# Moving activations and normed activations to other start addresses modulo 512 bytes

## The chip, the cores and the metric

The kernel runs on one core of a Trainium2 chip. The metric is the time of the kernel on the device, in microseconds (us). Before the change three runs took 1006.5, 1007.32 and 1007.83 us; the median is 1007.32.

SBUF, the on-chip memory, has 128 partitions. A tile of 128 x 512 numbers of 4 bytes takes 2048 bytes in each partition, and its address is the place of its first byte in the partition, the same in all 128. The change is about these addresses.

## The reference

A decoder trunk of two layers on 512 positions and 1024 channels, all in float32:

```
x = x + multiscale_pool(rmsnorm(x))           # layer 0
x = x + conv_ffn(rmsnorm(x))
k, v = split(rmsnorm(x, kv_norm) @ w_kv)      # layer 1
x = x + diff_attention(rmsnorm(x), k, v)
x = x + conv_ffn(rmsnorm(x))
return rmsnorm(x, final_norm)

def conv_ffn(h):                              # 1024 -> 2 x 2816 -> 1024
    u = causal_dwconv(h @ w_up)               # width 3
    a, g = split(u)
    return (silu(g) * a) @ w_down
```

The two feed-forward parts hold most of the arithmetic: each multiplies 512 x 1024 by 1024 x 5632 and 512 x 2816 by 2816 x 1024.

## The kernel before

A float32 product is made of three products of halves: every operand is split into a high part that TensorE's one-pass format (fp32r) holds exactly and a low part with the rest, and `mm3` (L159 to L163) adds high x high (L161), high x low (L162) and low x high (L163) into one PSUM bank. In `nc.tensor.matmul(ps, l, r)` the operand `l` is stationary: its 128 columns are loaded into the array by a weight load (PEld in the profile). `r` is moving: its columns stream through. In the profile's names, `pu<-n1h,hi_u`, the moving operand stands first and the stationary one second.

The stages, in order, with the tiles of their matmuls:

- Pooling of layer 0 (`dps`, `pp`): 128 and 256 columns.
- Up projections (`pu`, in `product`): for each of 44 blocks of 128 channels, 8 x 3 matmuls; the weights `hi_u`, `lo_u` are stationary, the normed, transposed activations `n1h`, `n1l` (layer 1: `n3h`, `n3l`) move, 512 columns each. The first four blocks are computed in two halves of 256 columns.
- Down projections (`pd`, in `ffn`): the activations `ah`, `al` are stationary, the weights `hi_d`, `lo_d` move, 512 columns each.
- Attention: values `pv` (weights move, normed activations `n2h`, `n2l` are stationary), queries and keys `pj_q`, `pj_k` (weights stationary, normed activations move), scores `sc`, transposes `pa`, weighted values `po`, output projection `pw` (weights move, activations `oh`, `ol` stationary).

Weights come in chunks of 512 KB: a DMA on SP's queue into `raw` (three buffers), ScalarE's copy into `hi`, VectorE's subtraction into `lo` (five buffers each). The order of the instructions of each engine is the order in which the code issues them; the early part follows a written list of steps (`ORDER`).

Tiles come from pools, which take space in SBUF in the order in which they are opened. With the sizes of their tiles this gives the addresses, in bytes in the partition:

| pool | what is in it | starts at | its tiles modulo 512 |
|---|---|---|---|
| start | `ones`, 896 bytes | 1152 | 128 |
| tp | 44 tiles of 2048 bytes: activations `ah`, `al`, `oh`, `ol`, `qs`, `kh`, `kl`, `v`, pooling operands | 2048 | 0 |
| hp | 2 tiles of 16384 bytes: normed activations | 92160 | 0 |
| wp | 13 tiles of 4096 bytes: weights `raw`, `hi`, `lo` | 124928 | 0 |
| const | x, identity, gains | 178176 | x and identity 0 |
| work | scratch | 196928 | 2048-byte tiles 0, 4096-byte tiles 320 |

Every matmul operand in tp, hp and wp is a slice that begins a multiple of 512 bytes into its tile (128 columns of 4 bytes, or more). So it has its tile's residue modulo 512: before the change 0 for both operands of every product that `mm3` makes.

Of the kernel before, what the change touches and what calls it, by code (L numbers as in the profile page):

```python
# [8 lines left out]
F32 = mybir.dt.float32  # L9
# [5 lines left out]
P = 128  # L15
# [48 lines left out]
def trunk(ctx, tc, x, norm_g, pool_w, pool_scale, kv_norm, w_kv, wq, lam, subln_g, wo,  # L64
          w_up, conv_w, conv_b, w_down, final_norm, consts, out):
    nc = tc.nc

    start = ctx.enter_context(tc.tile_pool(name="start", bufs=1))
    tp = ctx.enter_context(tc.tile_pool(name="tp", bufs=1))
    hp = ctx.enter_context(tc.tile_pool(name="hp", bufs=1))  # L70
    wp = ctx.enter_context(tc.tile_pool(name="wp", bufs=1))
    const = ctx.enter_context(tc.tile_pool(name="const", bufs=1))
    work = ctx.enter_context(tc.tile_pool(name="work", bufs=1))
    ones = start.tile([P, 224], F32, name="ones")
    psum = ctx.enter_context(tc.tile_pool(name="psum", bufs=8, space=bass.MemoryType.PSUM))
    ctx.enter_context(tc.manual_schedule(engines={mybir.EngineType.PE}))

# [59 lines left out]
    for i in (1, 2):  # L137
        n = S if i == 1 else 64
# [623 lines left out]
```

## Time and profile before

| | |
|---|---|
| median of three runs | 1007.32 us |
| profiled execution | 1007.95 us |
| its span | 1006.2 us |
| granted TensorE clock, mean | 0.999 |
| PE busy | 991.4 us, 99% |
| weight loads (PEld) busy | 838.3 us, 83% |
| VectorE, ScalarE, GpSimd busy | 569.7, 426.9, 85.7 us |
| DMA, mean | 95 GB/s |

The page of the profile gives shares over the whole span. A busy PE says little, since matmuls overlap: a row's duration runs from the start to a modelled end, and the next one has started long before. What a matmul costs in a row of matmuls is the distance from its start to the next start. The timeline has the starts, and the table by stretches the counts.

### The profile page before, as it was taken

The numbers are of one execution on the slowest core, as the hardware profiler recorded it, in microseconds if no ns is written. First come the engines' busy times: TensorE is split into PE (matmuls) and PEld (weight loads), VectorE is DVE, ScalarE is ACT, GpSimd is POOL, SyncE is SP. The second block draws the span as 40 slices with busy tenths as digits, with TensorE's granted clock in tenths as the row PEclk, the third lists the DMA queues.
The fourth block names the chain that finished last, engine by engine and source line by source line (L and its number), as shares of the span: only waits on it lengthen the run. The fifth ranks groups of instructions, "written<-read, shape, count | busy, mean of one in ns | idle before, by whom it ended". The sixth has DMA issues, their size and how long they took to land.

```text
span 1006.2 us, 12339 instructions
## 1 busy us (share of the span) xinstructions
PE 991.4 (99%) x4870; PEld 838.3 (83%) x4870; DVE 569.7 (57%) x872; ACT 426.9 (42%) x671; POOL 85.7 (9%) x113
## 2 busy tenths in 40 slices
PE   8999999999999999999999999999999999999997
PEld 8998888888888888778888887988888888888885
DVE  5766656656632323557766797576566566532213
ACT  5554443444432213446756662464444434422211
POOL 4500000000000001261220101000000000000001
PEclk9999999999999999999999999999999999999999
DMA  7333233233232321243213111243332332332312
GB/s 259 109 105 105 85 104 101 88 105 94 94 110 85 114 98 49 71 139 105 64 42 105 64 43 42 84 126 95 94 105 88 101 104 85 105 94 95 105 42 83
DMA packets 128707, 95.33 MB, mean 95 GB/s; under 512 B 3329, under 2 KB 111498, under 8 KB 128650
## 3 DMA queue, kind: packets, MB, share of 16 engines
q1 hardware_dynamic: 128650, 94.55, 30.4%
q8 instruction: 38, 0.62, 0.2%
q14 instruction: 19, 0.16, 0.0%
HBM read 92.44 MB, written 2.10 MB: 94 GB/s over the span
## 4 chain that ended last, share of the span: by engine, by line
PE 96%; DVE 1%; DMA 1%; ACT 0%; issue 0%; SPq 0%; POOL 0%; DVEq 0%; POOLq 0%; ACTq 0%
PE pu L161 16%; PE pu L162 16%; PE pu L163 16%; PE pd L163 8%; PE pd L161 8%; PE pd L162 8%; PE sc L531 2%; PE po L560 2%; PE pw L163 1%; PE pj_k L161 1%; PE pj_k L162 1%; PE pw L162 1%; PE pw L161 1%; PE pj_k L163 1%; PE pj_q L162 1%; PE pj_q L161 1%
## 5 line engine op out<-in xcount | busy, mean ns | idle before, releaser
L144 DVE TENSOR_TENSOR lo_u<-raw_u,hi_u 128x1024 fp32r<-128x1024 f32 x84 | 103.3, 1232 | 126.9 <-ACT hi_u L143 126.7
L161 PE MATMUL pu<-n3h,hi_u 128*128 128x512 f32 (+1 forms) x384 | 142.9, 372 | 0.0
L161 PE MATMUL pu<-n1h,hi_u 128*128 128x512 f32 (+1 forms) x384 | 142.8, 372 | 0.0
L162 PE MATMUL pu<-n3l,hi_u 128*128 128x512 f32 (+1 forms) x384 | 142.6, 371 | 0.0
L162 PE MATMUL pu<-n1l,hi_u 128*128 128x512 f32 (+1 forms) x384 | 142.6, 371 | 0.0
L163 PE MATMUL pu<-n1h,lo_u 128*128 128x512 f32 (+1 forms) x384 | 142.6, 371 | 0.0
L163 PE MATMUL pu<-n3h,lo_u 128*128 128x512 f32 (+1 forms) x384 | 142.6, 371 | 0.0
L144 DVE TENSOR_TENSOR lo_d<-raw_d,hi_d 128x1024 fp32r<-128x1024 f32 x44 | 53.9, 1226 | 147.1 <-ACT hi_d L143 147.1
L161 PE MATMUL pd<-hi_d,ah 128*128 128x512 f32 x352 | 137.0, 389 | 0.0
L163 PE MATMUL pd<-hi_d,al 128*128 128x512 f32 x352 | 136.9, 389 | 0.0
L162 PE MATMUL pd<-lo_d,ah 128*128 128x512 f32 x352 | 136.9, 389 | 0.0
L143 ACT CAST hi_u<-raw_u 128x1024 fp32r<-128x1024 f32 x84 | 88.1, 1051 | 64.2 <-PE pu L162 59.4
L143 ACT CAST hi_d<-raw_d 128x1024 fp32r<-128x1024 f32 x44 | 46.2, 1050 | 142.0 <-PE pd L163 131.3
L161 PEld LDWEIGHTS pu<-n1h,hi_u 128*128 128x128 f32 x384 | 72.3, 188 | 12.6
L163 PEld LDWEIGHTS pu<-n3h,lo_u 128*128 128x128 f32 x384 | 72.3, 188 | 12.6
L163 PEld LDWEIGHTS pu<-n1h,lo_u 128*128 128x128 f32 x384 | 72.3, 188 | 12.5
L162 PEld LDWEIGHTS pu<-n3l,hi_u 128*128 128x128 f32 x384 | 72.4, 188 | 12.5
L161 PEld LDWEIGHTS pu<-n3h,hi_u 128*128 128x128 f32 x384 | 72.3, 188 | 12.4
L162 PEld LDWEIGHTS pu<-n1l,hi_u 128*128 128x128 f32 x384 | 72.4, 188 | 12.3
L162 PEld LDWEIGHTS pd<-lo_d,ah 128*128 128x128 f32 x352 | 66.1, 188 | 13.7
L163 PEld LDWEIGHTS pd<-hi_d,al 128*128 128x128 f32 x352 | 66.1, 188 | 13.7
L161 PEld LDWEIGHTS pd<-hi_d,ah 128*128 128x128 f32 x352 | 66.1, 188 | 13.6
(146 smaller groups left out, 1553.2 us busy)
## 6 DMA issues: line engine op xcount, KB each, us to landing
raw_u<-in_w_up_dram SPq DMA_DIRECT2D x88, 512.0 KB, 3.7
raw_d<-in_w_down_dram SPq DMA_DIRECT2D x44, 512.0 KB, 3.3
raw_v<-in_w_kv_dram SPq DMA_DIRECT2D x8, 512.0 KB, 3.6
raw_q<-in_wq_dram SPq DMA_DIRECT2D x8, 512.0 KB, 4.0
raw_k<-in_w_kv_dram SPq DMA_DIRECT2D x8, 512.0 KB
raw_o<-in_wo_dram SPq DMA_DIRECT2D x8, 512.0 KB, 4.9
x<-in_x_dram SPq DMA_DIRECT2D x4, 512.0 KB
out_dram<-y SPq DMA_DIRECT2D x8, 256.0 KB, 2.1
```

Of the source, the lines that this page charges most:

```text
L143: nc.scalar.copy(hi, src)
L144: nc.vector.tensor_tensor(lo, src, hi, ALU.subtract)
L161: nc.tensor.matmul(ps, lh, rh, start=first, stop=False)
L162: nc.tensor.matmul(ps, lh, rl, start=False, stop=False)
L163: nc.tensor.matmul(ps, ll, rh, start=False, stop=last)
L531: nc.tensor.matmul(ps[:, :m], qs[h, c][:, q], k[:, :m], start=not last, stop=bool(last))
L560: nc.tensor.matmul(po[h][:, qi * P:(qi + 1) * P], aT[:, kt * P:(kt + 1) * P], vt[kt][h // 4][:, (h % 4) * VD:(h % 4 + 1) * VD], start=kt = ...
```

## The change

The pools are opened in another order, and two pools of one tile each stand between them: 256 bytes (64 numbers) and 288 bytes (72 numbers). The two tiles are filled with zeros on GpSimd, and nothing reads them.

```diff
     start = ctx.enter_context(tc.tile_pool(name="start", bufs=1))
+    wp = ctx.enter_context(tc.tile_pool(name="wp", bufs=1))
+    gap1 = ctx.enter_context(tc.tile_pool(name="gap1", bufs=1))
     tp = ctx.enter_context(tc.tile_pool(name="tp", bufs=1))
+    gap2 = ctx.enter_context(tc.tile_pool(name="gap2", bufs=1))
     hp = ctx.enter_context(tc.tile_pool(name="hp", bufs=1))
-    wp = ctx.enter_context(tc.tile_pool(name="wp", bufs=1))
     const = ctx.enter_context(tc.tile_pool(name="const", bufs=1))
     work = ctx.enter_context(tc.tile_pool(name="work", bufs=1))
     ones = start.tile([P, 224], F32, name="ones")
+    for pool, n in ((gap1, 64), (gap2, 72)):
+        nc.gpsimd.memset(pool.tile([P, n], F32, name="gap"), 0.0)
```

The addresses after it: wp at 2048 (0 modulo 512), tp at 55552 (256), hp at 145952 (32), const at 178720 (x and identity 32), work at 197472 (its 2048-byte tiles 32, its 4096-byte tiles 352). For the products this means:

| product | moving, from | stationary, from | before, moving / stationary | after |
|---|---|---|---|---|
| pu, pj_q, pj_k | hp | wp | 0 / 0 | 32 / 0 |
| pv | wp | hp | 0 / 0 | 0 / 32 |
| pd, pw | wp | tp | 0 / 0 | 0 / 256 |
| pp, sc | tp | tp | 0 / 0 | 256 / 256 |
| po | tp | work | 0 / 0 | 256 / 32 |

The instructions of PE, VectorE, ScalarE and SP are the same in the same order, with the same waits. Only GpSimd's row of instructions changes, at its beginning. Before:

```order
L757 UNCONDITIONAL_BRANCH
L109 MEMSET halfneg 128x8
L181 ISA
L181 TENSOR_SCALAR r_n_150<-ssq_n_148 128x1
L184 TENSOR_TENSOR r_n_150<-r_n_150,halfneg 128x1
```

And after it (`gap` are the new tiles, `halfneg` a constant for the power -0.5, `r_n` the factor of the first normalization; the lines are 5 further down):

```order
L762 UNCONDITIONAL_BRANCH
L79 MEMSET gap 128x64
L79 MEMSET gap 128x72
L114 MEMSET halfneg 128x8
L186 ISA
L186 TENSOR_SCALAR r_n_160<-ssq_n_158 128x1
```

The two fills stand ahead of the fill of `halfneg`; the rest follows as before.

## The prediction

> **What bounds the kernel now.** I read the page first: the share of each engine and the chain that ended last.
>
> ```profile
> span 1006.2 us, 12339 instructions
> PE 991.4 (99%) x4870; PEld 838.3 (83%) x4870; DVE 569.7 (57%) x872; ACT 426.9 (42%) x671; POOL 85.7 (9%) x113
> ...
> PE 96%; DVE 1%; DMA 1%; ACT 0%; issue 0%; SPq 0%; POOL 0%; DVEq 0%; POOLq 0%; ACTq 0%
> ```
>
> TensorE sets the end: 96% of the chain is matmuls following each other on PE. So the time is the number of matmuls times the distance from one start to the next, plus little else. Next the table by stretches, for two long stretches: first the up projections of layer 0, then its down projections (columns: stretch, PE busy and count, weight loads, DVE, ACT, POOL, granted clock, DMA share, GB/s).
>
> ```profile
> 70.00:290.00 220.00, 220.00 (x973) 182.21 (x972) 134.47 (x167) 94.81 (x121) 0.00 (x0) 1.00 0.32 97
> 290.00:385.00 95.00, 95.00 (x421) 78.69 (x420) 24.49 (x24) 19.48 (x20) 0.00 (x0) 1.00 0.31 103
> ```
>
> PE is never idle, the granted clock is full (1.00), DVE is busy 61% of the first stretch (134.47 of 220) and 26% of the second, ACT 43% and 21%, DMA a third. Nothing else is near a limit. The count gives the distance of starts: 220/973 = 226 ns and 95/421 = 226 ns (a matmul that straddles an edge is counted too). The timeline gives it exactly. The first and last rows stand here of 19 matmuls of 512 columns, and then 22 of 256 columns:
>
> ```profile
> 199.78 0.39 PE L162 MATMUL pu<-n1l,hi_u 128*128 128x512 f32 x1
> ...
> 203.86 0.39 PE L162 MATMUL pu<-n1l,hi_u 128*128 128x512 f32 x1
> ```
> ```profile
> 59.05 0.28 PE L162 MATMUL pu<-n1l,hi_u 128*128 128x256 f32 x1
> ...
> 61.57 0.28 PE L162 MATMUL pu<-n1l,hi_u 128*128 128x256 f32 x1
> ```
>
> 18 steps in 4.08 us are 226.7 ns each; 21 steps in 2.52 us are 120.0 ns each. (The 389 ns in the groups is one matmul's length from start to modelled end; neighbours overlap, so it is not what one costs.) The two sizes separate a part per column from a part per matmul: (226.7 - 120.0)/256 = 0.417 ns a column, and 226.7 - 512 x 0.417 = **13.3 ns per matmul that does not depend on its columns**. All the change can win lies in these 13.3 ns.
>
> What are they? One thing happens once per matmul whatever its width: the next stationary block, 128 columns of 4 bytes, is read from SBUF while the moving operand is read. The timeline shows both starting together:
>
> ```profile
> 200.24 0.39 PE L161 MATMUL pu<-n1h,hi_u 128*128 128x512 f32 x1
> 200.24 0.19 PEld L162 LDWEIGHTS pu<-n1l,hi_u 128*128 128x128 f32 x1
> ```
>
> So two streams leave SBUF at the same moment, and before the change both begin at 0 modulo 512. Whether they get into each other's way is the open question; no matmul of 256 columns or more in this trace has its two operands at different residues, so the trace can't answer it directly. One thing speaks for it. The distance isn't a constant of the array: after each pause of a stream it is longer for a while, with the same tiles. Eight starts just after a group of score matmuls:
>
> ```profile
> 520.50 0.39 PE L162 MATMUL pv<-lo_v,n2h 128*128 128x512 f32 x1
> 520.73 0.40 PE L163 MATMUL pv<-hi_v,n2l 128*128 128x512 f32 x1
> 520.97 0.39 PE L161 MATMUL pv<-hi_v,n2h 128*128 128x512 f32 x1
> 521.20 0.40 PE L162 MATMUL pv<-lo_v,n2h 128*128 128x512 f32 x1
> 521.43 0.39 PE L163 MATMUL pv<-hi_v,n2l 128*128 128x512 f32 x1
> 521.66 0.39 PE L161 MATMUL pv<-hi_v,n2h 128*128 128x512 f32 x1
> 521.89 0.39 PE L162 MATMUL pv<-lo_v,n2h 128*128 128x512 f32 x1
> 522.12 0.39 PE L163 MATMUL pv<-hi_v,n2l 128*128 128x512 f32 x1
> ```
>
> Seven steps in 1.62 us are 231.4 ns, 4.7 over the settled 226.7. An overhead that depends on how two streams stand to each other in time is what a clash at the memory looks like, and a shift of addresses acts on the same thing. A fixed cost of changing the weights would not do this.
>
> **The change part by part.** It adds two fills on GpSimd, moves addresses, and leaves the instructions of all other engines as they are, in the same order with the same waits.
>
> (a) The two fills stand ahead of the fill of halfneg on POOL:
>
> ```profile
> 0.72 0.10 POOL L109 MEMSET halfneg<- 128x8 f32 x1 [0.29 <-POOLq L745]
> 5.45 0.22 POOL L181 TENSOR_SCALAR r_n<-ssq_n 128x1 f32<-128x1 f32 x1 [4.63 <-ACT sq_n L191]
> ```
>
> POOL then idles 4.63 us for the first row of x, so two fills of 64 and 72 columns, at the 0.10 us of an 8-column one or even at several times that, are hidden by that wait. Without it they would cost some 0.2 us. I take 0.
>
> (b) The tensors other than TensorE's operands (x, the gains, scratch) begin 32 bytes later. VectorE and ScalarE keep their work; if they became a few per cent slower, the 39% and 57% that they have free in the up stretch would hold it. I take 0.
>
> (c) The matmuls whose two operands now differ modulo 512. Their counts, from the groups by line with shapes kept apart:
>
> ```profile
> L161 PE MATMUL pd<-hi_d,ah 128*128 128x512 f32 x352 | 137.0, 389 | 0.0
> L161 PE MATMUL pu<-n1h,hi_u 128*128 128x512 f32 x320 | 124.5, 389 | 0.0
> L161 PE MATMUL pw<-hi_o,oh 128*128 128x512 f32 x64 | 25.6, 400 | 0.8 <-ACT oh L148 0.8
> L161 PE MATMUL pv<-hi_v,n2h 128*128 128x512 f32 x64 | 25.2, 394 | 0.0
> L161 PE MATMUL pj_k<-n2h,hi_k 128*128 128x512 f32 x64 | 25.0, 391 | 0.0
> L161 PE MATMUL pj_q<-n2h,hi_q 128*128 128x512 f32 x64 | 25.0, 390 | 0.0
> L161 PE MATMUL pu<-n1h,hi_u 128*128 128x256 f32 x64 | 18.3, 286 | 0.0
> ```
>
> Each row stands three times (the three products of the hi and lo halves), and pu in both layers. That makes pu 2 x 3 x 320 = 1920 of 512 columns and 2 x 3 x 64 = 384 of 256, with the moving operand 32 bytes off; pj_k and pj_q 384, likewise 32; pv 192, where the stationary one is 32 off; pd 3 x 352 = 1056 and pw 192, where the stationary one is 256 off. Together 4128. The pooling products and the scores have both operands in the activations' pool: their relation stays 0, and I take 0 for them. The small attention products and transposes are paced by their weight loads (below), and I take 0.
>
> What does one of the 4128 gain? The lower end of the gain is nothing, or less (a rival below). The upper end comes from the transposes, 128 columns each:
>
> ```profile
> 32.22 1.75 PE pt_n L226 x16
> ```
>
> 1.75/16 = 109.4 ns each, where 128 columns at 0.417 would need 53: here the weight load sets the pace, so one load takes at most 109.4 ns. A matmul of 256 columns can't follow faster than its weight load and so gains at most 120.0 - 109.4 = 10.6 ns, and I take this end for 512 columns too, since the overhead was the same. Between 0 and 10.6 no row decides; I take half of the 13.3, 6.7 ns, as if the two streams met half as often. The settled distance would be 220.0 ns.
>
> As to the skill: in "TensorE: Matmul & The Clock Gate", section "Back-to-back issue gap", the Trainium skill gives N/2.4 + 2.5 ns for one matmul after another. By that figure an estimate of the distance is 215.8 ns at 512 columns and 109.2 at 256, the gain 10.9 x 3744 + 10.8 x 384 = 45 us and the time 962 us. The trace agrees with its part per column (0.417), not with its constant (13.3 against 2.5).
>
> The sum: pu 1920 x 6.7 ns = 12.9 us; pd 1056 x 6.7 = 7.1; pj, pv and pw 768 x 6.7 = 5.1; pu with 256 columns 384 x 6.7 = 2.6. Together 27.7 us. The profiled execution took 1007.95 us (its span 1006.2 and 1.75 around it), which is 0.6 over the median of 1007.32. 1007.95 - 27.7 = 980.2; against the median **979.6 us**. With the upper end it is 4128 x 10.6 = 43.8 us, or 963.5.
>
> Would something else become the bound at 220 ns? Everything that runs beside a matmul stays the same in total: DVE's 134.47 us would stand in a stretch of 213.5 instead of 220, 63%. No.
>
> **The rivals.**
>
> 1. *Addresses don't matter; the 13.3 ns is the price of swapping weights.* For it: in the settled rhythm 226.7 is the same in the up and the down stretch, though moving and stationary tiles change places there. Against it: the 231.4. The time is 1007.3. The Trainium skill speaks for this rival: "TensorE: Matmul & The Clock Gate", section "Step-by-step: what each phase is for", says that TensorE reads the moving operand and the weights through two separate SBUF ports, and that loading the next weights takes nothing from the running matmul. By that rule the change does nothing. No row here contradicts it outright; the shifting distance makes me doubt it.
>
> 2. *Only one shift helps.* The normed activations move by 32 bytes, the others by 256, so the two groups can differ. If only the 256 helps (pd and pw, 1248): 1248 x 6.7 = 8.4 us, 998.9. If only the 32 helps (pu, pj and pv, 2880): 19.3 us, 988.0. For it: a shift of 32 bytes is a small part of the 512 bytes that a weight load reads. Against it: no row tells the two apart.
>
> 3. *Slower: the streams no longer settle.* That the distance falls back to 226.7 after a pause may need equal residues. If the streams with shifted operands stay in the state that they have after a pause, each of the 4128 takes 4.7 ns more: 19.4 us, 1026.7. If only pd and pw do (1248): 5.9 us, 1013.2. It decides once the mean distance is over 227.2 ns (2 us over 4128 matmuls). For it: 231.4 occurs, over and over. Against it: it is always a passing state.
>
> **How the numbers follow.** Within 0.2% (2 us) a change of this kernel can't be told from none. I give the forecast, both shifts help by something up to 10.6 ns, 0.38; rival 2, 0.20; rival 1, 0.25; rival 3, 0.17. Faster is 0.38 + 0.20 = 0.58, same 0.25, slower 0.17. The forecast's own range is 962 to 993 (a gain of 3.5 to 11 ns each). To hold 8 in 10 the range takes in rivals 2 and 1 and the smaller form of rival 3: 962 to 1013; left out are the larger form of rival 3 (about 0.11) and a gain beyond the upper end (0.04). The likeliest case gives 979.6, rounded 980.
>
> **What would show it.** In the profile after, starts of pu with 512 columns 220.0 ns apart (18 steps in 3.96 us), those of 256 columns 113.3, and pd the same 220.0; the up stretch then holds about 3% more matmuls in the same time. Scores and pooling products keep their distance. Rival 1 would show 226.7 everywhere; rival 2 one of pu and pd at 226.7 and the other below it; rival 3 one of them over 227.2 for a whole stage. The sum would be wrong if PE showed new idle time ahead of the matmuls, or if the time moved while the distances did not.

## The result: slower, and only where the shift is 32 bytes

The changed kernel takes 1020.5 us (median of four runs), the kernel before beside it 1006.91: a ratio of 1.013, with an interval of 1.0115 to 1.0144. That is 13.6 us more. The forecast was 27.7 us less.

The profile after, first the page:

```profile
span 1018.2 us, 12341 instructions
...
PE 1006.1 (99%) x4870; PEld 836.3 (82%) x4870; DVE 568.2 (56%) x872; ACT 427.4 (42%) x671; POOL 86.2 (8%) x115
...
PE 97%; DVE 1%; DMA 1%; SPq 0%; issue 0%; ACT 0%; DVEq 0%; POOLq 0%; POOL 0%; ACTq 0%
```

The kernel is bound as before; no new wait has come up. The table by stretches, for the same two stretches:

```profile
70.00:290.00 220.00, 220.00 (x945) 176.84 (x944) 131.25 (x161) 92.01 (x118) 0.00 (x0) 1.00 0.32 96
290.00:385.00 95.00, 95.00 (x421) 78.67 (x420) 25.45 (x28) 21.10 (x22) 0.00 (x0) 1.00 0.30 99
```

The columns are those of the prediction's table. In 220 us the up projections now get through 945 matmuls; it was 973. The down projections get through 421, as before. PE is full in both and the granted clock is 1.00, so the matmuls of `pu` themselves stand further apart. The timeline has the distance: first and last of 19 `pu` matmuls of 512 columns, of 19 `pd` matmuls, and of 20 `pu` matmuls of 256 columns.

```profile
199.70 0.39 PE L168 MATMUL pu<-n1h,lo_u 128*128 128x512 f32 x1
...
203.90 0.39 PE L168 MATMUL pu<-n1h,lo_u 128*128 128x512 f32 x1
...
329.79 0.39 PE L167 MATMUL pd<-lo_d,ah 128*128 128x512 f32 x1
...
333.87 0.39 PE L167 MATMUL pd<-lo_d,ah 128*128 128x512 f32 x1
```
```profile
58.66 0.28 PE L167 MATMUL pu<-n1l,hi_u 128*128 128x256 f32 x1
...
60.87 0.28 PE L168 MATMUL pu<-n1h,lo_u 128*128 128x256 f32 x1
```

18 steps of `pu` in 4.20 us are 233.3 ns (before 226.7). 18 steps of `pd` in 4.08 us are 226.7, unchanged. 19 steps of 256 columns in 2.21 us are 116.3 (116.6 by the starts in ns; before 120.0). So where the 32 bytes were put, the matmuls of 512 columns became slower and those of 256 faster, and where the 256 bytes were put, nothing changed. That the shift is the cause is what the experiments below test.

The loss adds up. From all starts in the two traces (distances with a wait or pause in them left out), 1920 `pu` matmuls of 512 columns take 6.6 ns more each, 12.7 us; 576 of `pj_q`, `pj_k` and `pv` go from 228.0 to 233.1 on average, 2.9 us; 384 `pu` matmuls of 256 columns go from 119.9 to 117.0, 1.1 us less. Together 14.5 us, against 13.6 measured (11.6 to 14.5 by the interval). The spans of the two traces differ by less, 12.0 us, because waits of PE differ too: before, PE is idle for 1.9 us ahead of `pv<-hi_v,n2l`, and in the trace after for none. Of the kernels below that keep the time of before, two have this wait (1.6 and 1.9 us) and one has 0.1, so it is not the change's.

### The profile page after: what moved, and what is told of

Same layout as the page of the kernel before. It is cut to its first block, busy times and chain, and to the rows that moved or that the text cites. A ratio compares the mean times of both kernels' runs of the same rounds, so it can differ in the third digit from the quotient of the medians.

```text
span 1018.2 us, 12341 instructions
## 1 busy us (share of the span) xinstructions
PE 1006.1 (99%) x4870; PEld 836.3 (82%) x4870; DVE 568.2 (56%) x872; ACT 427.4 (42%) x671; POOL 86.2 (8%) x115
## 4 chain that ended last, share of the span: by engine, by line
PE 97%; DVE 1%; DMA 1%; SPq 0%; issue 0%; ACT 0%; DVEq 0%; POOLq 0%; POOL 0%; ACTq 0%
PE pu L166 16%; PE pu L167 16%; PE pu L168 16%; PE pd L168 8%; PE pd L167 8%; PE pd L166 8%; PE sc L536 2%; PE po L565 2%; PE pv L168 1%; PE pw L168 1%; PE pv L167 1%; PE pj_k L167 1%; PE pj_k L166 1%; PE pv L166 1%; PE pj_k L168 1%; PE pw L166 1%
```

## The experiments

Theory A: what counts is how the moving and the stationary operand stand to each other modulo some power of two; 32 bytes is a bad relation, 256 is as good as 0. The rivals: the loss comes from the activations at 256 or from the scratch that moved along (B); an operand that begins at 32 is read more slowly by itself (C); traffic of the other engines makes the difference (D). The first six kernels are edits of the kernel before, all with the same means: the order of the pools, gaps between them and the size of the first tile. The code shown leaves out the lines that fill the gaps; its comments are added.

### The normed activations alone at 32

```diff
     start = ctx.enter_context(tc.tile_pool(name="start", bufs=1))
+    wp = ctx.enter_context(tc.tile_pool(name="wp", bufs=1))
     tp = ctx.enter_context(tc.tile_pool(name="tp", bufs=1))
+    gap1 = ctx.enter_context(tc.tile_pool(name="gap1", bufs=1))     # 8 numbers, 32 bytes
     hp = ctx.enter_context(tc.tile_pool(name="hp", bufs=1))
-    wp = ctx.enter_context(tc.tile_pool(name="wp", bufs=1))
```

> Weights and activations at 0 modulo 512, normed activations alone at 32. Theory A (what counts is how the moving operand stands to the stationary one that is loaded meanwhile; only the 32 hurts): pu, pj and pv of 512 columns at 233 ns as after the change, pd and pw at 226.7, pu of 256 columns at 117; about 1020 us, the whole loss. Theory B (the loss comes from the activations at 256, or from scratch and constants that moved with them): under 1010 us. Both have scratch and constants 32 bytes off here as after the change, so a loss here with nothing else doesn't yet separate A from a shift of scratch; the next kernel does.

1021.63 us, ratio 1.0142 (1.0125 to 1.0159). The timeline of this kernel, first and last of 19 matmuls each:

```profile
199.69 0.39 PE L166 MATMUL pu<-n1h,lo_u 128*128 128x512 f32 x1
...
203.89 0.39 PE L166 MATMUL pu<-n1h,lo_u 128*128 128x512 f32 x1
...
329.77 0.39 PE L165 MATMUL pd<-lo_d,ah 128*128 128x512 f32 x1
...
333.85 0.39 PE L165 MATMUL pd<-lo_d,ah 128*128 128x512 f32 x1
```

`pu` at 4.20/18 = 233.3 ns, `pd` at 226.7: the whole loss is here. Scratch and constants stand 32 bytes further on here too, as after the change; the third kernel takes up that rival.

### The activations alone at 256

```diff
+    wp = ctx.enter_context(tc.tile_pool(name="wp", bufs=1))
+    gap1 = ctx.enter_context(tc.tile_pool(name="gap1", bufs=1))     # 256 bytes
     tp = ctx.enter_context(tc.tile_pool(name="tp", bufs=1))
+    gap2 = ctx.enter_context(tc.tile_pool(name="gap2", bufs=1))     # 256 bytes
     hp = ctx.enter_context(tc.tile_pool(name="hp", bufs=1))
-    wp = ctx.enter_context(tc.tile_pool(name="wp", bufs=1))
```

> Activations at 256, normed activations and weights at 0, scratch and constants at the residues they had before the change. Theory A: nothing slower, pd at 226.7 ns, pu at 226.7, 1007 us within 2. Theory B (the 256 costs): 1013 us or more, although pd already kept 226.7 in the changed kernel.

1007.01 us, ratio 0.9996 (0.9982 to 1.0009). Its stretches hold the counts of the kernel before:

```profile
70.00:290.00 220.00, 220.00 (x973) 182.15 (x972) 135.76 (x168) 96.25 (x123) 0.00 (x0) 1.00 0.33 97
290.00:385.00 95.00, 95.00 (x421) 78.67 (x420) 23.60 (x22) 18.53 (x19) 0.00 (x0) 1.00 0.32 103
```

Theory B falls as far as the 256 bytes go.

### Everything 32 bytes later

```diff
-    ones = start.tile([P, 224], F32, name="ones")
+    ones = start.tile([P, 232], F32, name="ones")
```

(with the pools in the order start, wp, tp, hp)

> Everything 32 bytes later: weights, activations and normed activations all at 32 modulo 512, so the relation of every pair of operands is 0 as before the change. Theory A (relation of the two): pu and pd at 226.7 ns, 1007 us within 2. Theory C (an operand that begins off a boundary of 64 or more bytes is read more slowly by itself): pu at 233 and pd above 226.7 too, about 1027 us.

1006.08 us, ratio 0.9989 (0.9977 to 1.0).

```profile
70.00:290.00 220.00, 220.00 (x973) 182.15 (x972) 134.44 (x167) 95.05 (x121) 0.00 (x0) 1.00 0.33 97
```

973 again. An operand at 32 is not slow by itself, and scratch and constants, which moved by 32 here too, cost nothing: theory C falls, and the rest of B. What counts is how the two operands stand to each other, their relation.

### Three other places

The gap ahead of `hp` of the first experiment, with 16 numbers (64 bytes) in place of 8:

> The normed activations at 64 modulo 512, weights and activations at 0. If the streams alone (relation 64: 229.05 ns at 512 columns, 117.75 at 256; relation 192, which pv has: 233.35) give the kernel's time: pu 1920 x 2.4 ns = 4.5 us, pj 384 x 1.5 = 0.6, pv 192 x 5 = 1.0, the 256-column products 384 x -2.2 = -0.9; together +5.2, 1012 us. If any shift off 0 costs the same as 32: 1021.

1013.07 us, ratio 1.005 (1.0031 to 1.0068): +5.0 us, where the streams alone (below) had said +5.2.

```profile
70.00:290.00 220.00, 220.00 (x963) 180.53 (x962) 134.08 (x167) 95.37 (x123) 0.00 (x0) 1.00 0.32 97
```

The same gap with 64 numbers (256 bytes):

> The normed activations at 256, weights and activations at 0. From the streams alone (relation 256: 226.6 ns at 512 columns, 120 at 256): pu at 226.7, 1007 us within 2. If normed activations off 0 are slow whatever the shift: 1020.

1007.96 us, ratio 1.0008 (0.9996 to 1.0021).

```profile
70.00:290.00 220.00, 220.00 (x973) 182.23 (x972) 134.90 (x168) 95.16 (x122) 0.00 (x0) 1.00 0.32 97
```

The normed activations can be moved by 256 bytes without loss; it is the 32, and less the 64, that hurts.

And the pools in the order start, wp, hp, a gap of 8 numbers, tp, so that the 32 bytes stand between the operands of `pd` and `pw`:

> The activations at 32, weights and normed activations at 0: the 32 bytes now sit between the operands of pd and pw. From the streams alone (stationary 32 off: 233.3 ns): pd 1056 x 6.6 ns = 7.0 us, pw 192 x 5 = 1.0; 1015 us, pu at 226.7. If the loss belongs to the normed activations and not to the 32 bytes: 1007.

1013.95 us, ratio 1.0078 (1.0056 to 1.0101): +7.9 by the ratio, 7.2 by the medians (8.0 expected). The stretches show that the loss has moved to the down projections:

```profile
70.00:290.00 220.00, 220.00 (x971) 182.08 (x970) 135.42 (x168) 95.66 (x123) 0.00 (x0) 1.00 0.32 97
290.00:385.00 95.00, 95.00 (x408) 76.59 (x408) 23.61 (x22) 18.18 (x18) 0.00 (x0) 1.00 0.29 97
```

408 matmuls of `pd` in place of 421: 95/408 = 233 ns.

### The streams by themselves

A kernel that leaves the trunk out: it loads x, makes one large moving and one large stationary tile (fp32r, and the same again in bf16, a type of 2 bytes), and runs 42 matmuls in each stream, with one relation of the two start addresses. It ran once.

```
def stream(n, a, b, ...):            # a, b: offsets in numbers (4 bytes each, bf16 2)
    for i in range(COUNT):
        o, w = a + i % 7 * S, b + i % 15 * P
        nc.tensor.matmul(ps[:, :n], stay[:, w:w + P], move[:, o:o + n], ...)
```

> Not the trunk: a kernel of matmul streams alone, 42 matmuls each, one relation of the two operands after another, with the other engines idle; the output is not the reference's. Theory A: 512 columns give 226.7 ns with relation 0, 233 with 32 bytes whichever of the two is shifted, 226.7 with 256, and 226.7 where both are shifted alike (32/32, 256/256); 256 columns give 120.0 at 0 and 117 at 32; between these the distance is a function of the relation that repeats with a period of at most 256 bytes. Theory C: 32/32 is as slow as 32/0. Theory D (other engines' traffic makes the difference): 512 columns give one distance, the same for all relations, since the other engines rest. For bf16 operands: if the 13.3 ns per matmul are the price of reading 512 bytes of weights beside the moving operand, bf16 has about half of it (220 ns at 512 columns); if they are a fixed price of swapping weights, 226.7 again.

Five rows of its timeline; in each a part of one stream is merged into one row (start, time from the first start to the last modelled end, count). In order: fp32r of 512 columns with the moving operand 32 bytes off, 256 bytes off, both operands 32 bytes off; bf16 of 512 columns with relation 0 and 32.

```profile
54.67 6.22 PE L103 MATMUL t<-move,stay 128*128 128x512 f32 x26
...
132.92 5.85 PE L103 MATMUL t<-move,stay 128*128 128x512 f32 x25
...
249.81 5.85 PE L103 MATMUL t<-move,stay 128*128 128x512 f32 x25
...
434.68 5.77 PE L103 MATMUL t<-moveb,stayb 128*128 128x512 bf16 x26
...
443.75 5.77 PE L103 MATMUL t<-moveb,stayb 128*128 128x512 bf16 x26
```

Take the last matmul's length off (0.39, for bf16 0.38): 5.83/25 = 233 ns at 32, 5.46/24 = 227 or 228 at 256 and where both are shifted alike, 5.39/25 = 216 for bf16 at either relation. The starts themselves, over the end of each stream, give these distances (the moving operand shifted; good to about 0.3 ns):

| relation, bytes | 512 columns, ns | 256 columns, ns |
|---|---|---|
| 4 | 235.4 | 123.3 |
| 16 | 231.7 | 113.4 |
| 32 | 233.4 | 116.7 |
| 48 | 230.0 | 118.4 |
| 64 | 229.1 | 117.8 |
| 96 | 233.4 | 120.1 |
| 128 | 233.4 | 118.7 |
| 192 | 233.4 | 113.3 |
| 256 | 226.6 | 120.0 |
| 320 | 228.7 | 117.8 |
| 32 / 32 and 256 / 256 | 226.7 | not run |

Relation 0 isn't in the table: at 512 columns it was the first stream, which starts slowly and reaches 226.7 ns over its last twelve steps (226.7 again at the end of the next two kernels), and at 256 columns it has 120.0. With the stationary operand shifted instead, 32 bytes give 233.3, 256 give 226.7, and 128 and 384 give 232.6 and 232.1, some 1 ns under the 233.4 of the moving one. At 512 columns the streams from 256 to 480 bytes that have a partner 256 bytes lower agree with it within 0.3 ns.

With the other engines at rest the picture is that of the trunk, so theory D falls. At 384 columns 32 bytes change nothing (173.3 at 0, 32, 64 and 256; 176.0 at 128). And bf16 knows no relation: 215.8 ns at all five that were run, and 109.2 at 256 columns. That answers my question about its constant: about 2.5 ns per matmul in place of 13.3. So the 13.3 are not a price of swapping weights that every type of operand pays, and with bf16 it isn't half either.

### A finer map, and smaller weight blocks

```
TESTS = [("r", 512, a, 0, P) for a in range(0, 64)]
TESTS += [("r", 256, a, 0, P) for a in range(0, 128, 4)]
TESTS += [("r", n, a, 0, c) for n in (512, 256) for c in (128, 96, 64, 32) for a in (0, 8)]
```

> Again matmul streams alone, 36 matmuls each, output not the reference's: 512 columns with the moving operand 0, 4, 8, ... 252 bytes off, 256 columns 0, 16, ... 496 bytes off, and then stationary blocks of 128, 96, 64 and 32 columns at relations 0 and 32. If the extra time comes from the weight load reading the same memory as the moving operand, it shrinks with the columns of the stationary block: 13.3 ns at 128, about 7 to 8 at 64, about 5 at 32, and the difference between relations 0 and 32 shrinks alike. If it is a fixed price of swapping float32 weights, 13.3 ns at every size. In the map no relation at 512 columns is expected under 226.7 ns; one that is would give a faster kernel.

No relation between 4 and 252 bytes lies under 228.9 ns at 512 columns; the worst (20, 68, 88, 100, 116, 132 and 196 bytes) stand at 240.0. At 256 columns the values from 256 to 496 bytes repeat those from 0 to 240 within 0.1 ns: the period is 256 bytes, not 512. But streams at one relation can have two rhythms: 16 bytes gave 113.4 ns at 256 columns in the first kernel of streams and 118.7 here, 48 bytes 230.0 and 233.4 at 512. In the first kernel 448 bytes gave 117.8 at 256 columns where 192 gave 113.3; here both give 113.3. What decides which rhythm a stream falls into isn't shown.

The smaller weight blocks, relation 0 and 512 columns, with 128, 96, 64 and 32 stationary columns:

```profile
688.90 4.70 PE L102 MATMUL t<-move,stay 128*128 128x512 f32 x20
...
705.51 4.76 PE L102 MATMUL t<-move,stay 128*96 128x512 f32 x20
...
722.19 4.76 PE L102 MATMUL t<-move,stay 128*64 128x512 f32 x20
...
738.80 4.80 PE L102 MATMUL t<-move,stay 128*32 128x512 f32 x20
```

20 matmuls take longer with less to load: by the starts 226.7, 229.9, 230.0 and 231.7 ns, while the rows of the weight loads themselves get shorter, 189, 161, 134 and 108 ns. With relation 32 it is 233.4, 233.3, 230.7, 233.3. At 256 columns and relation 0 the same kernel has it the other way: 120.0, 116.0, 113.4 and 117.8 ns, so smaller blocks are faster there, though not in order of their size. My expectation that the extra time shrinks with the bytes of the weight load holds at neither width, and a fixed price doesn't either.

### Pairs, and other places for hi and lo

```
ALTERNATE = [((0,), (0,)), ((0, 8), (0, 8)), ((0, 8), (8, 0)), ((0, 8), (0,)), ((0,), (0, 8)), ...]
TESTS += [(512, (rh, rl, rh), (0, 0, ll)) for ll in (0, 16, 32, 48) for rh in (0, 16, 32, 48) for rl in (0, 16, 32, 48)]
```

> Matmul streams alone, 36 of 512 columns each, output not the reference's. First nine streams in which residues alternate from matmul to matmul. With moving 0, 32, 0, 32 and stationary 0, 32, 0, 32 a matmul and its own weights have relation 0, and the weights loaded while it runs have relation 32; with stationary 32, 0, 32, 0 it is the other way round. If what counts is the load that runs meanwhile, the first gives 233 ns and the second 226.7; if it is a matmul's own pair, the first gives 226.7 and the second 233; if moving operands that follow each other must agree, both give 233. Then 64 patterns like mm3's three products, with 0, 64, 128 or 192 bytes for low weights, high and low moving parts: if one lies under 226.7 ns, a kernel with other places for hi and lo can beat the kernel before; from the maps so far I expect none to.

In the two streams in question, the one with a matmul and its own weights alike and the one with a matmul and the weights loaded meanwhile alike, 22 matmuls each, and then the stream with everything at 0:

```profile
21.92 5.30 PE L97 MATMUL t<-move,stay 128*128 128x512 f32 x22
...
30.32 5.26 PE L97 MATMUL t<-move,stay 128*128 128x512 f32 x22
...
88.66 5.15 PE L97 MATMUL t<-move,stay 128*128 128x512 f32 x22
```

By the starts 233.7, 231.7 and 226.7 ns. Neither pair alone sets the distance: with the moving operands alternating, both are slow, as the third reading had it, but a stationary operand that alternates while the moving one stays at 0 gives 230.1 too. In these streams the 226.7 came only where all operands stood alike. Of the 64 patterns of hi and lo parts the one with everything at 0 is the fastest, at 226.7; the others lie between 228.8 and 235.5. So the kernel before already has the best places that these maps contain for its 512-column products. By the streams alone the 256-column products could gain up to 6.7 ns each (113.3 at 192 bytes), 384 of them 2.6 us, an estimate; the same relation modulo 256 had 117.8 in one stream, they read the same normed tiles as the 512-column ones, and another place for their weights alone wasn't tried.

## Why the prediction was wrong

- **What bounds the kernel**: right. PE sets the end, a gain or loss per matmul goes straight to the time, and the 14.5 us worked out from the distances agree with the 13.6 measured.
- **"All the change can win lies in these 13.3 ns"**: the reading of 0.417 ns a column and 13.3 per matmul holds at equal residues (384 columns fit it too, with 173.3 ns), and bf16 with 2.5 shows that not every type pays these 13.3. What fp32r pays them for isn't shown. I turned a bound on the gain into an expectation of one; at 512 columns no run won any of it.
- **Part (c), the step that failed**: "I take half of the 13.3, 6.7 ns, as if the two streams met half as often." This supposes that equal start addresses are a bad relation. They are the best of the map for 512 columns: 226.7, every other relation below 256 bytes about 229 or more. The 6.7 ns gained became 6.6 lost for `pu` (and about 5 for `pj` and `pv`), 0 for `pd` and `pw`, and 3.0 gained for the 256-column products.
- **The 231.4 ns after a pause** was read as a sign that there is something to win. The same row says only that a stream that isn't settled is slower. The streams alone bear that out: with both operands at 32 the first twelve steps average 228.9 ns and the rest 226.7. With 32 bytes between the operands a stream settles too, but at 233.3. Why isn't shown.
- **Parts (a) and (b)**: right. The kernel with everything 32 bytes later, where scratch and constants move too, is at 0.9989 (0.9977 to 1.0). The kernel with the activations at 256 has two fills as well and is at 0.9996 (0.9982 to 1.0009), so the fills cost nothing that the time shows.
- **Rival 1** (addresses don't matter, 0.25): wrong for fp32r: the distance went from 226.7 to 233.3 ns with the addresses alone. What the Trainium skill says of two separate read ports ("TensorE: Matmul & The Clock Gate", "Step-by-step: what each phase is for") fits the bf16 streams, 215.8 ns at every relation; whether the ports have to do with what fp32r shows is open. The Trainium skill's N/2.4 + 2.5 ns (same page, "Back-to-back issue gap") gives 215.8 at 512 columns and 109.2 at 256, and the bf16 streams have 215.8 and 109.2. The section calls it the gap of an isolated matmul and has about 131 ns for a stream at 512 columns; no stream here comes near that. For fp32r at 512 columns the formula is 10.9 ns or more too short.
- **Rival 2** (one of the two shifts, 0.20): right that they differ; but neither helps 512 columns. That 32 is "a small part of the 512 bytes that a weight load reads" was no argument: 32 cost more than 64 and 256.
- **Rival 3** (the streams no longer settle, 0.17): right in the sign and in that equal residues are the good ones, not in the mechanism: the streams do settle, and not in the state after a pause (231.4), but at 233.3. I priced it at 4.7 ns from that passing state; it is 6.6 for `pu`. I put its smaller form on `pd` and `pw`, where the shift is the larger one; they lost nothing, and `pu`, `pj` and `pv` lost. Its full form, 1026.7, counted 1248 matmuls of `pd` and `pw` that kept their pace. With the 2496 matmuls of 512 columns that did lose it would have been 11.7 us at 4.7 ns, which comes near the 13.6 partly by luck, since it also leaves out the 1.1 us that the 256-column ones gained.
- **The range** of 962 to 1013 had 45 us of room below 1007.3 and 6 above. The measured 1020.5 lies between the two forms of rival 3 (1013.2, at the very end of the range, and 1026.7), where it had no room. The trace had no row with unequal operands, and a sign that rests on no row should have had equal room on both sides.

## What to carry to other kernels

Where TensorE is full with fp32r matmuls, read the distance from start to start, not the duration: 6.6 ns on 226.7 was nearly the whole effect and no wait showed it. Where the matmuls have 512 columns, keep all operands of such a stream at the same residue modulo 256 bytes; here 32 bytes between the operands' pools were enough to lose 1.3%. At 256 columns the rule doesn't hold: equal residues have 120.0 ns there, among the slower values of the map, and at 384 columns 32 and 64 bytes changed nothing. Measure the width that you have. And when a trace shows one relation only, it says nothing about which way another one goes: a kernel of streams alone, half a millisecond long, gives an answer for dozens of places at once, though not to the last nanosecond, as the two rhythms show.

## What the runs showed of the hardware

- The distance of fp32r matmuls depends on the start addresses of moving and stationary operands relative to each other, with a period of 256 bytes as far as the two rhythms allow: 226.7 ns at 0 and 256, up to 240.0 in between (512 columns). Shifting both alike changes nothing (226.7 at 32/32).
- At 256 columns the order is another: 120.0 at 0, 113.3 at 192 bytes, 123.3 at 4 (192 bytes modulo 256 had 117.8 in one stream).
- bf16 matmuls have no such dependence: 215.8 ns at 512 columns and 109.2 at 256 for every relation that was run.
- Fewer stationary columns do not help at relation 0 and 512 moving columns: 226.7 ns with 128, 231.7 with 32. At 256 moving columns they do: 120.0 with 128, 113.4 with 64, 117.8 with 32.
- What stays open is the mechanism. It isn't a matmul's own pair alone, nor the load that runs meanwhile alone, and it doesn't go in order of the bytes loaded; some relations have two rhythms. These runs show where it is fast, not why.
